# The second layer's rotation table, made in the first layer's expert stage

## The chip, the cores and the metric

The kernel runs on one core of one Trainium2 chip. Its engines are TensorE (PE in the profile, its weight loads PEld), VectorE (DVE), ScalarE (ACT), GpSimd (POOL) and SyncE (SP, which issues nearly all DMAs). Each engine takes its instructions strictly in the order in which they stand in its queue. The metric is device time in microseconds (us); lower is better. Before the change three runs took 1702.73, 1703.41 and 1704.15 us, a median of 1703.41 us.

## The reference

Two layers work on 256 latent tokens (`x`) and 256 context tokens (`ctx`), width 1024. Each layer has a mixer (three parallel parts: an S5 state-space scan, latent attention and a Hyena long convolution) and then a mixture of 32 SwiGLU experts, of which each token goes to two:

```python
for i in range(DEPTH):                       # DEPTH = 2
    u, cq, ckv, kr, hz = split(modulate(x, norm1_g[i], ...) @ w_in[i])
    s5  = s5_mixer(u, lam[i], b[i], c[i])    # h[t] = lam_bar*h[t-1] + bu[t], complex, both directions
    mla = mla_mixer(cq, ckv, kr, ...)
    hy  = hyena_mixer(hz, filters[i])
    x   = x + gate * (merge_groups(s5, mla, hy) @ w_out[i])
    x   = x + gate2 * hier_moe(modulate(x, norm2_g[i], ...), w1[i], w3[i], w2[i])
return rms_norm(x, final_g)
```

`lam_bar = exp(lam * dt)` depends on weights alone, and so do its powers. The second layer returns only the latent tokens.

## The kernel before

Every 128x1024 buffer is a "page" out of a pool of 44. Both mixers are written as Python generators that are woven into each other: each `yield` hands over to the next generator, and a scheduler, which works from a simulated timeline, then fixes every engine's queue. The expert stage is different: it stands inside a region with a manual schedule (`moe`, from L1763 on), where the instructions stay in the order in which they are written.

**The scan and its table.** `s5_scan` (L855 to L874) works on chunks of eight tokens, 64 chunks for each of 16 groups. It turns the complex recurrence into a real one: the driving values are multiplied by a table of rotations (cosines and sines, two pages), scanned with real decays `rho` (one page), and turned back. `s5_rotation` makes these. First, from the angle's cosine and sine, it squares and renormalises small 128x2x16 tiles eight times (`square`, L473 to L475, three DVE instructions; `unit`, L339 to L342, four, after six of the squarings), and squares the magnitude three times (L487). Then it doubles the table five times (L503 to L508), six DVE instructions for each length, 2 to 32 for each of the 16 groups, so 32 to 512 elements a partition. One ACT copy spreads the decays over the `rho` page. All of it hangs on weights alone.

**Where it is called.** Each mixer weaves four generators, named by letters in `first`: r the rotation, d the drive matrices (`expand`, L436 to L445 on DVE, whose results PE transposes at L460), c the scan's input chunks, a the inputs of the attention (L789, L939). In the first mixer the order of the letters is 'rdca', in the second 'acrd', with d empty there: the second layer's drive matrices are made earlier, in the first layer's expert stage.

**The expert stage of the first layer.** For each of 32 experts, 12 pages of weights (512 KB each) come in through SP; PE multiplies 64 gathered tokens by eight of them (`first_half`, L1586), ACT and DVE make SwiGLU of it (L1592 on DVE), PE turns it (`turn`, L1601) and multiplies by the other four (`second_half`, L1610), ACT and DVE scale the result (L1722), and PE adds it back to the tokens (`combine`, L1692), with a DVE addition into `xT` for each bank of PSUM (`residual`, L1624). A comparison (L1873) makes the matrix of ones and zeros that the next `combine` needs. After the 32 experts comes one more block for an expert with over 64 tokens (`first_half(X1, pages)`), then the last additions (`combine_last`, L1702), and a loop over further such blocks whose count is read from memory (L1905).

**Steps for the second layer in this stage.** `next_weights` chains generators of the second layer, and the stage takes one step of it twice for each expert from the seventh on (`NAHEAD` is 6). What is left after the 32nd expert is taken at once by `for _ in ahead: pass`. Between two `yield`s stands one step.

**The limit on weights ahead.** `ws.pump` says how many pages may be written into the program ahead of the page in use: 34 less the expert's number, but not under `NLAST`.

```python
            if e >= NAHEAD:
                next(ahead, None)      # stands twice in each expert
        for _ in ahead:                # after expert 31
            pass
        if i == 0:
            b = first_half(X1, pages)
```

Of the kernel before, what the change touches and what calls it, by code (L numbers as in the profile page):

```python
# [31 lines left out]
BIG = 1.0e30  # L32
NPAGE = 44
NEARLY = 5
NFIRST, NSTEP, NLAST, NAHEAD = 34, 1, 18, 6
PLAN = [
    {'lag': 2, 'ts': True, 'vs': False, 'nbank': (3, 3, 2), 'kvs': True,
     'qs': True, 'ps': True, 'order': 'ahsd', 'na': 1, 'ro': 2,
# [32 lines left out]
def build(tc, A, dbg=None):  # L71
# [8 lines left out]
    stage = ["z"]  # L80
# [209 lines left out]
    def layer_weights(i):  # L290

        V = {}
# [173 lines left out]
        def s5_rotation():  # L466

            stage[0] = "S5r"
            E = small([128, 6, 2, 16])
            mag = X["mag"]  # L470

            def square(d, a):
                nc.vector.tensor_mul(X["usq"][:, 0:2], a, a)  # L473
                nc.vector.scalar_tensor_tensor(d[:, 1], a[:, 0], 2.0, a[:, 1], op0=OP.mult, op1=OP.mult)
                nc.vector.tensor_sub(d[:, 0], X["usq"][:, 0], X["usq"][:, 1])  # L475

            e2 = small([128, 2, 16])
            e4 = small([128, 2, 16])
            square(e2, X["z"][:, 3:5])
            square(e4, e2)  # L480
            square(E[:, 0], e4)
            unit(E[:, 0])
            for n in range(5):
                square(E[:, n + 1], E[:, n])
                unit(E[:, n + 1])
            for _ in range(3):
                nc.vector.tensor_mul(mag, mag, mag)  # L487
            yield
            stage[0] = "S5r"
            T = [page(), page()]  # L490
            x = page()
            Tv = [t.rearrange("p (g s) -> p g s", g=16) for t in T]
            xv = x.rearrange("p (r g s) -> p r g s", r=2, g=16)
            nc.gpsimd.memset(Tv[0][:, :, 0:1], 1.0)
            nc.gpsimd.memset(Tv[1][:, :, 0:1], 0.0)
            for j in range(2):
                nc.vector.tensor_copy(Tv[j][:, :, 1:2], E[:, 0, j, :, None])
            for l in range(1, 6):
                n = 1 << l
                b_r, b_i = (E[:, l, j, :, None].to_broadcast([128, 16, n]) for j in range(2))  # L500
                a_r, a_i = Tv[0][:, :, 0:n], Tv[1][:, :, 0:n]
                o_r, o_i = Tv[0][:, :, n:2 * n], Tv[1][:, :, n:2 * n]
                nc.vector.tensor_mul(o_r, a_r, b_r)  # L503
                nc.vector.tensor_mul(xv[:, 0, :, 0:n], a_i, b_i)
                nc.vector.tensor_mul(o_i, a_r, b_i)
                nc.vector.tensor_mul(xv[:, 1, :, 0:n], a_i, b_r)
                nc.vector.tensor_sub(o_r, o_r, xv[:, 0, :, 0:n])
                nc.vector.tensor_add(o_i, o_i, xv[:, 1, :, 0:n])  # L508
            rho = page()
            rv = rho.rearrange("p (g s) -> p g s", g=16)  # L510
            act(rv, mag[:, :, None].to_broadcast([128, 16, 64]), AF.Copy)
            nc.gpsimd.memset(rv[:, :, 0:1], 0.0)
            V["rot"] = T
            V["rho"] = rho
            yield
# [64 lines left out]
        def s5_readout_matrices():  # L580
# [52 lines left out]
            for tau in range(8):  # L633
                for x in range(2):
# [6 lines left out]
                 readout=s5_readout_matrices)  # L641
# [106 lines left out]
    def mixer(i, acc):  # L748
# [10 lines left out]
        V = V_[i]  # L759
# [38 lines left out]
        def s5_chunks(u):  # L798

            stage[0] = "S5b"  # L800
            half = halves()
            Ut = [half(), half()]
            for t4 in range(2):
                b = bank(side=True)
                for t in range(4):
                    for m in range(2):
                        nc.tensor.matmul(b[64 * m:64 * m + 64, t * 128:(t + 1) * 128], u[m][:, t4 * 4 + t:512:8], ident,
                                         start=True, stop=True, tile_position=(0, 64 * m))
                bv = b.rearrange("p (t g h) -> p g t h", t=4, g=8)
                for g4 in range(2):  # L810
                    nc.scalar.copy(Ut[g4].rearrange("p (g t h) -> p g t h", g=4, t=8)[:, :, t4 * 4:t4 * 4 + 4, :],
                                   bv[:, g4 * 4:g4 * 4 + 4])
            yield
            stage[0] = "S5b"
            U = [half(), half()]
            for g4 in range(2):
                b = bank(side=True)
                for g in range(4):
                    nc.tensor.transpose(b[:, g * 128:(g + 1) * 128], Ut[g4][:, g * 128:(g + 1) * 128], ident)
                nc.scalar.copy(U[g4], b)  # L820
            V["U"] = U
            yield
# [461 lines left out]
        if i == 0:  # L1284
# [14 lines left out]
            spectrum = V["spectrum"]()  # L1299
# [8 lines left out]
        else:  # L1308
            rstd1 = rstd_of(None, D, acc=acc)
            first_projections(rstd1)  # L1310
            ahead(1)
        first = dict(r=V["rotation"], d=V["drive"] if i == 0 else lambda: iter(()), c=lambda: s5_chunks(V["u"]), a=attention_inputs)
        weave(*(first[c]() for c in pl["first"]), spectrum if i == 0 else iter(()))
        ro = V["readout"]() if i == 0 else iter(())
        n, mid = pl["ro"], pl["mid"]
# [89 lines left out]
    def moe(i, pctx, router, ws, last_part):  # L1405
# [394 lines left out]
        def next_weights():  # L1800

            V = V_[1]
            V["bank"] = lambda: pb("pX", 2)
            for name in ("spectrum", "powers", "readout", "drive"):
                for _ in V[name]():
                    stage[0] = "MOE"
                    yield
# [275 lines left out]
```

## Time and profile before

| | before |
|---|---|
| median of 3 runs | 1703.41 us |
| the profiled execution, its own time | 1700.06 us |
| its span, first to last instruction | 1698.2 us |
| PE, DVE, ACT, POOL busy | 1526.5, 890.3, 482.8, 95.6 us |
| mean granted TensorE clock | 0.955 of 2.4 GHz |
| DMA | 505.84 MB, mean 298 GB/s |

The profile's 40 slices of 42.5 us tell the stages apart. The first mixer lies in the first ten (DMA at 36 to 237 GB/s in most of them, PE and DVE taking turns), the first layer's experts in slices 10 to 21 (DMA at about 408 GB/s), the second mixer in slices 22 to 27 or so (36 to 300 GB/s, the granted clock down to six tenths in slice 22), the second layer's experts after that, again at 409 GB/s. The times in the rows are microseconds from the span's start; "[4.94 <-ACT MOEh L119]" at a row's end means that the engine was idle for 4.94 us before it, and that an ACT instruction at line 119 (the helper that issues all activations), writing MOEh, ended that. Names begin with the stage that made the tile: S5a, S5r and S5s for the scan, MOE for the experts, QKV and PROJ for the attention's inputs and the projections.

### The profile page before, as it was taken

What the parts mean: (1) busy time and instruction counts of PE and PEld (TensorE: products, weight loads), DVE (VectorE), ACT (ScalarE), POOL (GpSimd) and SP (SyncE); (2) the same over time, 40 slices, a digit from 0 to 9 for tenths busy, and PEclk for the clock granted to TensorE, in tenths of its full rate; (3) what the DMA queues carried; (4) which work ended last, traced back from release to release, by engine and by line L of the source; (5) the groups of instructions that cost most, each with busy time, mean ns of one, the idle gap of its engine ahead of it and who ended that gap; (6) DMA issues with size and microseconds to landing.
All of it is one profiled execution on the core that took longest, in us unless ns stands there. A gap on an engine that the chain in (4) does not pass through costs nothing. (4 is left out here: it accounts for less than half of the span.)

```text
span 1698.2 us, 22546 instructions
## 1 busy us (share of the span) xinstructions
PE 1526.5 (90%) x8073; PEld 785.7 (46%) x8073; DVE 890.3 (52%) x2180; ACT 482.8 (28%) x931; POOL 95.6 (6%) x154
## 2 busy tenths in 40 slices
PE   5888889997999999999999588898799999999985
PEld 1676744475433333344333477547444444333322
DVE  6769565555244546873744757455534444333233
ACT  3343545442111122111122534445311111111112
POOL 0000212002000000001100000010100000000000
PEclk9998899999999999999999698999899999999998
DMA  9111254659999999999999112578699999999994
GB/s 345 64 37 63 75 186 153 234 209 345 353 382 406 409 409 408 407 408 387 346 408 403 36 58 100 214 265 302 257 391 409 409 409 409 409 409 409 409 409 174
DMA packets 143300, 505.84 MB, mean 298 GB/s; under 512 B 19021, under 2 KB 19599, under 8 KB 142928
## 3 DMA queue, kind: packets, MB, share of 16 engines
q1 hardware_dynamic: 138736, 495.21, 75.6%
q0 software_dynamic: 4160, 8.61, 1.6%
q8 instruction: 66, 1.08, 0.3%
q10 hardware_dynamic: 288, 0.52, 0.1%
q14 instruction: 50, 0.41, 0.1%
HBM read 504.85 MB, written 3.64 MB: 299 GB/s over the span
## 5 line engine op out<-in xcount | busy, mean ns | idle before, releaser
L1586 PE MATMUL MOEp<-MOEpg,MOEpg 128*64 128x512 f32 x956 | 227.7, 603 | 13.6 <-DMA MOEpg<-in_w 12.4
L1722 DVE SCALAR_TENSOR_TENSOR MOEpg<-MOEpY,MOEwt,MOEpg 64x512 fp32r<-64x512 f32 x128 | 95.9, 749 | 243.6 <-ACT MOEpg L119 243.5
L1610 PE MATMUL MOEpY<-MOEpg,MOEhT 128*64 128x512 f32 x960 | 220.9, 602 | 1.8 <-DVE MOEhT L1602 1.8
L1586 PE MATMUL MOEp<-MOEpg,ROUTpg 128*64 128x512 f32 x960 | 215.5, 598 | 1.2 <-DMA MOEpg<-in_w 1.1
L1624 DVE SCALAR_TENSOR_TENSOR zxT<-MOEpC,zmod,zxT 128x256 f32<-128x256 f32 x385 | 168.1, 478 | 8.9 <-PE MOEpC L1702 2.8
L119 ACT ACTIVATE MOEpg<-MOEpY,MOEwt 64x512 fp32r<-64x512 f32 x128 | 87.4, 683 | 278.5 <-PE MOEpY L1610 220.5
L1592 DVE TENSOR_TENSOR MOEh<-MOEh,MOEp 128x256 f32<-128x256 f32 x65 | 27.3, 420 | 233.2 <-ACT MOEh L119 233.1
L1692 PE MATMUL MOEpC<-MOEGT,MOEpg 128*128 128x512 f32 (+1 forms) x496 | 130.1, 364 | 6.8 <-DVE zxT L1624 5.9
L119 ACT ACTIVATE MOEh<-MOEp 128x256 f32<-128x256 f32 x65 | 25.0, 385 | 388.5 <-PE MOEp L1586 388.5
L1586 PEld LDWEIGHTS MOEp<-MOEpg,MOEpg 128*64 128x64 f32 x956 | 59.2, 136 | 160.2 <-DMA MOEpg<-in_w 91.6
L1586 PEld LDWEIGHTS MOEp<-MOEpg,ROUTpg 128*64 128x64 f32 x960 | 65.5, 137 | 136.8 <-issue 105.2
L1610 PEld LDWEIGHTS MOEpY<-MOEpg,MOEhT 128*64 128x64 f32 x960 | 64.0, 137 | 121.6 <-issue 96.3
L1692 PEld LDWEIGHTS MOEpC<-MOEGT,MOEpg 128*128 128x128 f32 x496 | 75.2, 189 | 61.7 <-issue 26.0
L167 PE MATMUL ADAb<-ADApg,zcact 128*32 128x512 f32 x384 | 75.0, 614 | 12.2 <-DMA ADApg<-in_adaw 12.2
L789 PE MATMUL PROJb<-INPpg,PROJpg 128*128 128x512 f32 (+1 forms) x384 | 73.8, 356 | 6.4 <-DVE PROJpg L975 5.7
L789 PEld LDWEIGHTS PROJb<-INPpg,PROJpg 128*128 128x128 f32 x384 | 63.5, 206 | 15.9 <-ACT PROJpg L119 6.7
L119 ACT ACT_TABLE_LOAD x35 | 44.9, 1283 | 15.6 <-DVE ATTst L1103 5.7
L1661 PE MATMUL MOEpG<-MOEpg,ROUTpg 128*128 128x256 f32 x240 | 44.6, 310 | 1.1 <-DVE MOEpg L1496 1.1
L1661 PEld LDWEIGHTS MOEpG<-MOEpg,ROUTpg 128*128 128x128 f32 x240 | 33.0, 193 | 24.2 <-issue 15.8
L1374 PE MATMUL OUTb<-OUTpg,ATTpg 128*128 128x512 f32 (+1 forms) x192 | 39.1, 362 | 1.2 <-DVE ATTpg L231 1.2
L1092 PE MATMUL ATTb<-QKVpg,QKVpg 96*128 96x512 f32 x64 | 34.2, 637 | 6.5 <-ACT ATTpg L119 6.5
L1708 POOL TENSOR_TENSOR zxT<-zxT,MOEpg 128x512 f32<-128x512 f32 (+1 forms) x6 | 6.0, 1001 | 534.7 <-ACT MOEpg L119 534.6
(544 smaller groups left out, 2143.4 us busy)
## 6 DMA issues: line engine op xcount, KB each, us to landing
MOEpg<-in_w SPq DMA_DIRECT2D x719, 512.0 KB, 10.2
ADApg<-in_adaw SPq DMA_DIRECT2D x96, 512.0 KB, 6.9
ROUTpg<-in_w SPq DMA_DIRECT2D x61, 512.0 KB, 5.8
PROJpg<-in_win SPq DMA_DIRECT2D x16, 512.0 KB, 3.2
ATTpg<-in_wout SPq DMA_DIRECT2D x8, 512.0 KB, 3.3
OUTpg<-in_wout SPq DMA_DIRECT2D x8, 512.0 KB, 4.4
QKVpg<-in_uq SPq DMA_DIRECT2D x5, 512.0 KB, 3.3
MOEpg<-in_win SPq DMA_DIRECT2D x5, 512.0 KB, 10.1
```

What stands on the lines that cost most here:

```text
L119: nc.scalar.activation(out, in_, f, **kw)
L167: nc.tensor.matmul(b[q:q + 32, :], cact[:, k, :], w[:, h * 512:(h + 1) * 512], start=(k < 2), stop=(k >= KD - 2), tile_position=(0, q))
L789: nc.tensor.matmul(b, a_[:, c], b_[k][:, c0:], start=(first and n == 0), stop=(last and n == 2))
L1092: nc.tensor.matmul(b, qc[h][:, nq - NS + qt * 128:nq - NS + (qt + 1) * 128], kc[h], start=True, stop=True)
L1374: nc.tensor.matmul(b, a_[:, c], y_, start=(n == 0 and j == 0), stop=(n == KD - 1 and j == 2))
L1586: nc.tensor.matmul(b[64 * h:64 * h + 64, :], X[:, k, :], w[:, h * 512:(h + 1) * 512], start=(k == 0), stop=(k == KD - 1), tile_position=(0 ...
L1592: nc.vector.tensor_mul(h_, h_, b[:, 256:512])
L1610: nc.tensor.matmul(b[64 * h:64 * h + 64, :], hT[:, k % 2, (k // 2) * 64:(k // 2) * 64 + 64], w[:, h * 512:(h + 1) * 512], start=(k == 0), ...
L1624: nc.vector.scalar_tensor_tensor(xT[:, k, seg(s)], b[:, s * NS - c0:(s + 1) * NS - c0], mod[:, 40 + k, s:s + 1], xT[:, k, seg(s)], op0=OP. ...
L1661: nc.tensor.matmul(b[:, kk * 256:(kk + 1) * 256], hs[t][:, k * 128:(k + 1) * 128], G[:, t].rearrange("p e c -> p (e c)"), start=(t == 0 an ...
L1692: nc.tensor.matmul(b, Y_[p][j][rows, k * 128:(k + 1) * 128], GT_[p][rows], start=(j == 0), stop=(j == 1))
L1722: nc.vector.scalar_tensor_tensor(Y[1][rows_of, h * 512:(h + 1) * 512], b[rows], wt[rows], yh.bitcast(F32), op0=OP.mult, op1=OP.subtract)
```

## The change

`rotation` is added to the list that `next_weights` chains, at its end; the second mixer's r becomes empty. `s5_rotation` gets a `yield` ahead of each of five squarings and of each of the five doublings, which holds in the first mixer too. `NLAST` falls from 18 to 14.

```diff
--- before.py
+++ after.py
@@ -32,7 +32,7 @@
 BIG = 1.0e30
 NPAGE = 44
 NEARLY = 5
-NFIRST, NSTEP, NLAST, NAHEAD = 34, 1, 18, 6
+NFIRST, NSTEP, NLAST, NAHEAD = 34, 1, 14, 6
 PLAN = [
     {'lag': 2, 'ts': True, 'vs': False, 'nbank': (3, 3, 2), 'kvs': True,
      'qs': True, 'ps': True, 'order': 'ahsd', 'na': 1, 'ro': 2,
@@ -481,6 +481,8 @@
             square(E[:, 0], e4)
             unit(E[:, 0])
             for n in range(5):
+                yield
+                stage[0] = "S5r"
                 square(E[:, n + 1], E[:, n])
                 unit(E[:, n + 1])
             for _ in range(3):
@@ -496,6 +498,8 @@
             for j in range(2):
                 nc.vector.tensor_copy(Tv[j][:, :, 1:2], E[:, 0, j, :, None])
             for l in range(1, 6):
+                yield
+                stage[0] = "S5r"
                 n = 1 << l
                 b_r, b_i = (E[:, l, j, :, None].to_broadcast([128, 16, n]) for j in range(2))
                 a_r, a_i = Tv[0][:, :, 0:n], Tv[1][:, :, 0:n]
@@ -1309,7 +1313,7 @@
             rstd1 = rstd_of(None, D, acc=acc)
             first_projections(rstd1)
             ahead(1)
-        first = dict(r=V["rotation"], d=V["drive"] if i == 0 else lambda: iter(()), c=lambda: s5_chunks(V["u"]), a=attention_inputs)
+        first = dict(r=V["rotation"] if i == 0 else lambda: iter(()), d=V["drive"] if i == 0 else lambda: iter(()), c=lambda: s5_chunks(V["u"]), a=attention_inputs)
         weave(*(first[c]() for c in pl["first"]), spectrum if i == 0 else iter(()))
         ro = V["readout"]() if i == 0 else iter(())
         n, mid = pl["ro"], pl["mid"]
@@ -1801,7 +1805,7 @@
 
             V = V_[1]
             V["bank"] = lambda: pb("pX", 2)
-            for name in ("spectrum", "powers", "readout", "drive"):
+            for name in ("spectrum", "powers", "readout", "drive", "rotation"):
                 for _ in V[name]():
                     stage[0] = "MOE"
                     yield
```

Lines of the changed kernel are 2 to 4 higher than those of the kernel before.

**VectorE at the end of the first layer's experts.** Here L1722 and L1624 belong to expert 31, L1873 makes its matrix MOEGT, and the first L1592 after it is the SwiGLU product of the additional block, MOEh. Before:

```order
L1722 SCALAR_TENSOR_TENSOR MOEpg_6787<-MOEpY_6875,MOEwt_6137,MOEpg_6786 64x512 x2
L1624 SCALAR_TENSOR_TENSOR zxT_84<-MOEpC_6888,zmod_69,zxT_84 128x256 x2
L1873 TENSOR_SCALAR MOEGT_6893<-ziotaN_85,MOEidx_6135 128x512
L1592 TENSOR_TENSOR MOEh_6918<-MOEh_6918,MOEp_1469_6901 128x256
L1624 SCALAR_TENSOR_TENSOR zxT_84<-MOEpC_6922,zmod_69,zxT_84 128x256 x2
L1624 SCALAR_TENSOR_TENSOR zxT_84<-MOEpC_6927,zmod_69,zxT_84 128x256 x2
L1904 MEMSET MOEk_3290 128x1
```

Now, the same place up to the first instructions of the rotation (L473 to L475 are a squaring on S5a):

```order
L1726 SCALAR_TENSOR_TENSOR MOEpg_6779<-MOEpY_6869,MOEwt_6129,MOEpg_6778 64x512 x2
L1628 SCALAR_TENSOR_TENSOR zxT_84<-MOEpC_6888,zmod_69,zxT_84 128x256 x2
L1877 TENSOR_SCALAR MOEGT_6893<-ziotaN_85,MOEidx_6127 128x512
L473 TENSOR_TENSOR S5apg_3839<-S5apg_3839 128x32
L474 SCALAR_TENSOR_TENSOR S5apg_5075<-S5apg_3839 128x16
L475 TENSOR_TENSOR S5apg_5075<-S5apg_3839 128x16
L473 TENSOR_TENSOR S5apg_3839<-S5apg_5075 128x32
```

and where that ends (L511 and L512 close the last doubling, on S5r, L1596 is the SwiGLU product):

```order
L507 TENSOR_TENSOR S5rpg_6952<-S5rpg_6952,S5apg_5075 128x16x32
L508 TENSOR_TENSOR S5rpg_6954<-S5rpg_6953,S5apg_5075 128x512
L509 TENSOR_TENSOR S5rpg_6953<-S5rpg_6952,S5apg_5075 128x16x32
L510 TENSOR_TENSOR S5rpg_6954<-S5rpg_6953,S5apg_5075 128x512
L511 TENSOR_TENSOR S5rpg_6952<-S5rpg_6952,S5rpg_6954 128x16x32
L512 TENSOR_TENSOR S5rpg_6953<-S5rpg_6953,S5rpg_6954 128x16x32
L1596 TENSOR_TENSOR MOEh_7009<-MOEh_7009,MOEp_1473_6992 128x256
L1628 SCALAR_TENSOR_TENSOR zxT_84<-MOEpC_7013,zmod_69,zxT_84 128x256 x2
L1628 SCALAR_TENSOR_TENSOR zxT_84<-MOEpC_7018,zmod_69,zxT_84 128x256 x2
```

All 83 instructions of the rotation, 81 rows from L473 to L512, stand in one piece between MOEGT and the SwiGLU product of the additional block; none stands in an earlier expert.

**VectorE in the second mixer, ahead of the scan.** L231 is the low half of a projection's weights, L503 to L508 the last doublings, L855 the scan's first product, on S5s. Before:

```order
L231 TENSOR_TENSOR PROJpg_7672<-PROJpg_7669,PROJpg_7671 128x1024
L507 TENSOR_TENSOR S5rpg_7629<-S5rpg_7629,S5rpg_7631 128x16x16
L508 TENSOR_TENSOR S5rpg_7630<-S5rpg_7630,S5rpg_7631 128x16x16
L503 TENSOR_TENSOR S5rpg_7629<-S5rpg_7629,S5apg_5075 128x16x32
L505 TENSOR_TENSOR S5rpg_7630<-S5rpg_7629,S5apg_5075 128x16x32
L504 TENSOR_TENSOR S5rpg_7631<-S5rpg_7630,S5apg_5075 128x512
L506 TENSOR_TENSOR S5rpg_7631<-S5rpg_7630,S5apg_5075 128x512
L231 TENSOR_TENSOR PROJpg_7704<-PROJpg_7701,PROJpg_7703 128x1024
L507 TENSOR_TENSOR S5rpg_7629<-S5rpg_7629,S5rpg_7631 128x16x32
L508 TENSOR_TENSOR S5rpg_7630<-S5rpg_7630,S5rpg_7631 128x16x32
L855 TENSOR_TENSOR S5spg_7763<-S5spg_7735,S5rpg_7630 128x512
L856 TENSOR_TENSOR S5spg_7762<-S5spg_7735,S5rpg_7629 128x512
```

Now:

```order
L231 TENSOR_TENSOR PROJpg_7627<-PROJpg_7624,PROJpg_7626 128x1024
L231 TENSOR_TENSOR PROJpg_7672<-PROJpg_7669,PROJpg_7671 128x1024
L231 TENSOR_TENSOR PROJpg_7704<-PROJpg_7701,PROJpg_7703 128x1024
L862 TENSOR_TENSOR S5spg_7763<-S5spg_7735,S5rpg_6953 128x512
L859 TENSOR_TENSOR S5spg_7763<-S5spg_7735,S5rpg_6953 128x512
L860 TENSOR_TENSOR S5spg_7762<-S5spg_7735,S5rpg_6952 128x512
L861 TENSOR_TENSOR S5spg_7762<-S5spg_7735,S5rpg_6952 128x512
```

The doublings are gone; the scan's first products follow the weights' splits.

**VectorE in the first mixer.** L436 to L445 make the drive matrices, L503 to L508 (L507 to L512 in the changed kernel) double the table. Before, with the table's last doubling ahead of most of the drive matrices:

```order
L503 TENSOR_TENSOR S5rpg_655<-S5rpg_655,S5apg_292 128x16x32
L505 TENSOR_TENSOR S5rpg_656<-S5rpg_655,S5apg_292 128x16x32
L504 TENSOR_TENSOR S5rpg_657<-S5rpg_656,S5apg_292 128x512
L506 TENSOR_TENSOR S5rpg_657<-S5rpg_656,S5apg_292 128x512
L231 TENSOR_TENSOR PROJpg_720<-PROJpg_717,PROJpg_719 128x1024
L576 TENSOR_TENSOR PROJpg_649<-SPECpg_749,SPECb_653 128x512
L577 TENSOR_TENSOR PROJpg_649<-SPECpg_749,SPECb_653 128x512
L436 TENSOR_TENSOR SPECpg_757<-S5apg_292,S5apg_253 128x512
L438 TENSOR_TENSOR SPECpg_757<-S5apg_292,S5apg_253 128x512
L507 TENSOR_TENSOR S5rpg_655<-S5rpg_655,S5rpg_657 128x16x32
L508 TENSOR_TENSOR S5rpg_656<-S5rpg_656,S5rpg_657 128x16x32
L231 TENSOR_TENSOR PROJpg_765<-PROJpg_762,PROJpg_764 128x1024
```

Now, with the last drive matrices ahead of all but the first doubling:

```order
L437 TENSOR_TENSOR S5apg_550<-S5apg_292,S5apg_253 128x512
L438 TENSOR_TENSOR S5rpg_806<-S5apg_292,S5apg_253 128x512
L439 TENSOR_TENSOR S5apg_552<-S5apg_292,S5apg_253 128x512
L441 TENSOR_TENSOR S5apg_550<-S5apg_550,S5rpg_782 128x512
L445 TENSOR_TENSOR S5apg_552<-S5apg_552,S5rpg_782 128x512
L507 TENSOR_TENSOR S5rpg_799<-S5rpg_799,S5apg_292 128x16x2
L509 TENSOR_TENSOR S5rpg_800<-S5rpg_799,S5apg_292 128x16x2
L508 TENSOR_TENSOR S5rpg_801<-S5rpg_800,S5apg_292 128x16x2
L510 TENSOR_TENSOR S5rpg_801<-S5rpg_800,S5apg_292 128x16x2
L441 TENSOR_TENSOR S5apg_550<-S5apg_550,S5rpg_806 128x512
L445 TENSOR_TENSOR S5apg_552<-S5apg_552,S5rpg_806 128x512
L511 TENSOR_TENSOR S5rpg_799<-S5rpg_799,S5rpg_801 128x16x2
```

Before, the table's 32 instructions stood ahead of the last three of the four pairs of L441 and L445; now 26 of them stand behind the last pair.

## Rows read from the trace of the kernel before

**Rows 1.** Stretches: width, busy time by engine (instructions), PEclk, DMA share, GB/s.

```profile
900.00:920.00 20.00, 19.56 (x98) 8.08 (x96) 6.62 (x14) 4.40 (x8) 0.00 (x0) 1.00 1.03 409
...
940.00:960.00 20.00, 9.98 (x28) 7.49 (x28) 13.35 (x25) 12.93 (x21) 3.82 (x3) 0.50 0.05 15
```

**Rows 2.** Timeline of DVE, end of the first layer's experts: start, duration, instruction.

```profile
922.57 0.48 DVE L1873 TENSOR_SCALAR MOEGT<-ziotaN,MOEidx 128x512 fp32r<-128x512 f32 x1
927.98 0.42 DVE L1592 TENSOR_TENSOR MOEh<-MOEh,MOEp 128x256 f32<-128x256 f32 x1 [4.94 <-ACT MOEh L119]
928.32 1.65 DVE L1624 SCALAR_TENSOR_TENSOR zxT<-MOEpC,zmod,zxT 128x256 f32<-128x256 f32 x4
```

**Rows 3.** Timeline of PE, the same place.

```profile
927.45 1.19 PE L1692 MATMUL MOEpC<-MOEGT,MOEpg 128*128 128x512 f32 x4
929.33 0.70 PE L1692 MATMUL MOEpC<-MOEGT,MOEpg 128*128 128x512 f32 x2 [0.69 <-DVE zxT L1624]
...
932.52 3.65 PE L1610 MATMUL MOEpY<-MOEpg,MOEhT 128*64 128x512 f32 x16
...
940.74 2.04 PE L1702 MATMUL MOEpC<-MOEGT,MOEpg 64*128 64x512 f32 x4 [3.42 <-DVE zxT L1624]
```

**Rows 4.** Timeline of DVE, squarings of the second layer among the first layer's experts.

```profile
702.54 0.19 DVE L342 TENSOR_TENSOR S5apg<-S5apg,S5apg 128x32 f32<-128x32 f32 x1
702.76 0.19 DVE L473 TENSOR_TENSOR S5apg<-S5apg 128x32 f32<-128x32 f32 x1
...
703.20 0.19 DVE L339 TENSOR_TENSOR S5apg<-S5apg 128x32 f32<-128x32 f32 x1
...
703.84 0.19 DVE L342 TENSOR_TENSOR S5apg<-S5apg,S5apg 128x32 f32<-128x32 f32 x1
```

**Rows 5.** Stretches, instructions on the table (S5rpg) alone; both mixers.

```profile
77.00:98.00 21.00, 9.00 (x32) 1.05 (x1) 0.13 (x1) 1.00 0.08 27
...
1001.00:1015.00 14.00, 9.40 (x33) 1.05 (x1) 0.12 (x1) 0.98 0.20 71
```

**Rows 6.** Timeline of DVE, second mixer, the scan.

```profile
1014.43 0.69 DVE L855 TENSOR_TENSOR S5spg<-S5spg,S5rpg 128x512 f32<-128x512 f32 x1
...
1022.69 0.17 DVE L206 RECIPROCAL QKVrs<-QKVrs 128x4 f32<-128x4 f32 x1
```

**Rows 7.** Timeline of ACT, second mixer, ahead of the scan.

```profile
1005.63 1.05 ACT L119 ACTIVATE S5rpg<-S5apg 128x1024 f32<-128x1024 f32 x1
1006.58 1.99 ACT L119 ACTIVATE PROJpg<-PROJpg 128x1024 fp32r<-128x1024 f32 x2
1008.47 2.49 ACT L119 ACTIVATE S5spg<-S5sb 64x504 f32<-64x504 f32 x6
...
1014.18 0.26 ACT L119 ACTIVATE QKVrs<-QKVb,zeps 128x4 f32<-128x4 f32 x1 [2.05 <-PE QKVb L202]
```

**Rows 8.** Timeline of PE, second mixer, the same place.

```profile
1005.15 7.26 PE L841 MATMUL S5sb<-S5bpg,S5bpg 128*128 128x64 f32 x64
...
1022.91 1.11 PE L218 MATMUL QKVb<-zident,QKVrs 128*128 128x128 f32 x4 [8.77 <-DVE QKVrs L206]
```

**Rows 9.** Timeline of PE, first mixer, transposes of the drive matrices and what follows.

```profile
107.23 1.11 PE L460 MATMUL S5bb<-zident,S5apg 128*128 128x128 f32 x4 [3.34 <-DVE S5apg L441]
108.52 4.50 PE L460 MATMUL S5bb<-zident,S5apg 128*128 128x128 f32 x20 [0.18 <-DVE S5apg L441]
112.82 3.98 PE L841 MATMUL S5sb<-S5bpg,S5bpg 128*128 128x64 f32 x32
```

**Rows 10.** Timeline of DVE, first mixer, its first wait after that.

```profile
123.92 1.41 DVE L986 SCALAR_TENSOR_TENSOR S5bpg<-S5bpg,zchp,QKVb 128x512 f32<-128x512 f32 x2 [4.88 <-PE QKVb L218]
```

**Rows 11.** Stretch of the first mixer, columns as in the first group.

```profile
110.00:114.00 4.00, 4.00 (x24) 4.00 (x22) 0.00 (x0) 3.20 (x7) 0.00 (x0) 0.57 0.00 0
```

**Rows 12.** Waits of the weights' queue, 600 to 940 us: total, times, longest.

```profile
SPq L115 <- DMA MOEpg<-in_w: 229.9, 240, 4.0
...
SPq L115 <- PE MOEpY L1610: 4.3, 15, 0.4
```

## The prediction

> **What bounds the kernel now.** I read the slices of the page first: the first layer's experts and the second layer's run at about 409 GB/s, the mixers at far less. The windows then say what limits each stage. In the last experts of the first layer PE is busy 19.56 of 20 us while the DMA share is 1.03, and DVE only 6.62 [rows 1]: a page of 512 KB every 1.28 us (524288 bytes over 409 GB/s), twelve for an expert, 15.4 us an expert. The queue of the weights waits there 229.9 us in 240 pieces for transfers that it issued before, and 4.3 us in 15 pieces for the matmuls that free a page [rows 12]. So the experts are fed by memory, and small work on DVE beside them costs nothing as long as PE's inputs come in time. At the stage's end it is another matter. The weights have run out, the same two windows show the clock at half and DMA at 0.05 [rows 1], and every engine waits for one other in turn: a delay there is passed on in full. In both mixers PE, DVE and ACT take turns as well, and the waits in the timelines say who comes last.
>
> **Where the rotation goes.** The words of the change say "in steps among the experts". The queues say otherwise. The stage takes two steps in each of 26 experts (7 to 32), 52 in all, and the four generators that stood in the list before have 13, 8, 15 and 16 yields, 52 too. The rotation comes fifth, so none of its steps is reached, and all are emitted by the loop that empties the chain after expert 31. VectorE's queue shows 83 instructions in one piece between MOEGT and the SwiGLU product of the additional block. Queues are in order, so that product waits for all 83.
>
> **Term 1, the piece at the end of the experts.** Its length, from this trace: a squaring with its renormalising has seven instructions and takes 1.30 us (703.84 less 702.54), a bare squaring 0.44 (703.20 less 702.76) [rows 4]. Six of the first, two of the second and three squarings of the magnitude at 0.2 make 7.80 + 0.88 + 0.60 = 9.28 us. The table, 32 instructions, was busy 9.00 us in the first mixer, 9.40 with the scan's first instruction in the second [rows 5]; I take 9.0. Together 18.3 us. It starts where MOEGT ends (922.57 + 0.48 = 923.05) and ends at 941.3. The product started at 927.98 before, after 4.94 us of idle time on DVE that ACT's Silu ended [rows 2]: those 4.94 us hide part of the piece, the other 13.3 us do not. Nothing else hides it. Behind the product stand on DVE the additions into xT (L1624), for which PE's combine waits (0.69 us already), on PE the turn, second_half and the last combine [rows 3]; the SyncE loop (L1905) and the second mixer's normalisation follow from them.
>
> Then the clock. PE can do the first two banks of the combine and then stops for some 13 us. In the profile PE's clock is at half after waits far shorter than that: it waited 3.34 us in the first mixer, and 110 to 114 us were granted 0.57 [rows 9, 11]; after 3.42 us at the end of the experts [rows 3] the stretch was at 0.50 [rows 1]. So after 13 us of idleness the eight combine matmuls that stand from 929.33 to second_half (the first two are in a row) run at half clock, 0.51 us each as at 940.74 (2.04 over 4) instead of 0.30 as at 927.45 (1.19 over 4) [rows 3]: 8 x 0.21 = 1.7, less some 0.3 of PE's waiting between them that this fills (its 0.69 at 929.33 is one such wait), 1.4 us. In the first mixer the clock was at half from 107.23 to about 113.4 (0.57 over 4 us leaves 0.56 us at full speed), 6.2 us after PE's resumption [rows 9, 11]. Here second_half begins about 5 us after it, so about 1.2 of its 3.65 us [rows 3] are at half clock, 0.6 us. Term 1: 13.3 + 1.4 + 0.6 = **+15.3 us**. Ends: 13.0 with a table of 8.7 (9.40 less the 0.69 of L855 [rows 5, 6]) and no loss by the clock; 18.7 with the whole of second_half at half clock (13.3 + 1.7 + 3.65).
>
> A rule that speaks for a lower price stands in the Trainium skill, "Perfetto Trace Analysis", Identifying the Most-Contended Engine: for Vector the occupancy is a fair measure of how near the engine is to its limit. By it 18.3 us on an engine that is busy a third of the time would be free, and the term 0. The trace's row speaks against it at this place, since the idle time of the experts lies ahead of the piece in the queue; I give it the chance of rival B.
>
> **Term 2, the first mixer.** The new yields hold there too. The weaving takes one step from each generator in turn, and 26 of the table's 32 instructions now stand behind the drive matrices. PE waited 3.34 and 0.18 us for these (L441), and then ran 20 transposes in 4.30 us (112.82 less 108.52) at half clock [rows 9]. With the table behind, about 8 us of DVE work leave the way of L441; I keep 0.8 of the 3.52 us of waiting, as ACT's and DVE's first instructions of each matrix are still due, and gain 2.7. Without that wait the clock need not fall; the transposes then gain 1.9 (most of half of 4.30). Sum **-4.6 us**. DVE must be ready that much sooner for its next work behind PE; it waited 4.88 us there [rows 10], which covers it, barely. Ends: 0, if another wait takes its place, and -5.4 (3.52 + 1.9).
>
> **Term 3, the second mixer.** The table (9.0 us on DVE) and rho (1.05 on ACT [rows 7]) leave the stretch ahead of the scan. The scan started at 1014.43 behind the table, and PE waited 8.77 us for the reciprocal QKVrs, which stands behind the scan at 1022.69 [rows 6, 8]. What is late next: the scan's inputs are copied by ACT out of PSUM. These copies (2.49 us for six) began at 1008.47 behind two splits of 1.99 us that began at 1006.58, behind rho; without rho these begin at 1005.63 [rows 7], the copies about 0.95 sooner, and the chunks that the scan needs first are there about 1010.1 by the copies' pace and PE's L841, which runs until 1012.41 [rows 8]. The scan then starts 4.3 us sooner instead of 10, and so does the reciprocal, whose input is ready at 1014.18 [rows 7] and hence does not hold it. **-4.3 us**. Ends: 0, and -10.05, the whole of table and rho.
>
> **Edits at nothing.** The small squarings stood inside the experts before, where the scheduler had moved them; they leave 9.3 us of DVE work there, behind a stage fed by memory: 0, hidden as it was by the pages' pace. `NLAST` from 18 to 14 lets four pages fewer be written ahead in the last experts. The queue waits for transfers that are out already, not for its place in the program [rows 12], so 0; at the other end four pages of 1.28 us, +5.1, if each came late once. Gains below 0 have no source, since a shorter list ahead issues no page sooner.
>
> **Sum.** 15.3 - 4.6 - 4.3 = +6.4 us. Against the profiled execution, 1700.06 us (span 1698.2), this gives 1706.5; that execution lies 3.35 us below the median of 1703.41, so the forecast for a median is **1709.8 us**. The three terms' ends, not all at once, give 1705.5 to 1713.5 for this case.
>
> **Rivals.** A: the second mixer gives back the whole table and rho, 10.05 us instead of 4.3. For it: PE waits 8.77 us in one piece there and DVE is what it waits for [rows 6, 8]; against it: ACT's copies and L841 go on until after 1010 [rows 7, 8]. Sum 15.3 - 4.6 - 10.05 = +0.65: 1704.1 us, no change.
> B, the other side: the piece is hidden after all, as if it lay in DVE's idle time in the experts. For it: DVE is busy 6.62 of 20 us [rows 1]; against it: the order on DVE, with only 4.94 us of idle time behind MOEGT [rows 2]. Only -4.6 - 4.3 = -8.9 is left: 1694.5 us. It decides as soon as term 1 is under 5.5 us.
> C: the shorter limit on pages ahead makes PE wait for weights at the end of the stage, +5.1 more: 1714.9 us. For it: the stage has no slack at a DMA share of 1.03 [rows 1]; against it: the queue's waits [rows 12].
> D: both mixers only shift their waits, and term 1 stands alone: 1718.7 us. For it: DVE's cover in the first mixer is barely enough [rows 10], and after the scan comes the same chain as before; against it: two waits of PE (3.34 and 8.77) that end on instructions directly behind the table [rows 8, 9].
>
> **Chances.** The forecast 66%, of which 6 lie within 0.2% of before (3.4 us, about what a measurement of this kernel can tell from no change); A 13%, B 5%, C 8%, D 8%. Slower by more: 60 + 8 + 8 = 76%; within: 6 + 13 = 19%; faster: 5%. The range takes in A and half of C and leaves B and D out: 1702.5 to 1715.5 us.
>
> **What would show it.** Right: on DVE some 18 us of small S5a and S5r instructions behind MOEGT, the SwiGLU product about 13 us later, PE idle meanwhile and its clock at half at the turn; the experts as long as before and the same waits of the weights' queue; PE's wait for QKVrs at 4 to 5 us instead of 8.77; PE's wait for L441 under 1 us and the clock at full from 106 to 114 us. Wrong: the product no more than 5 us late (B), a stretch of PE waiting for pages after expert 25 (C), a wait of unchanged length under another name in a mixer (D), or the scan starting as soon as 1004 on the old scale (A).

## The result, and the profile after

The median rose from 1703.07 us (6 runs, 1700.58 to 1704.15) to 1710.23 us (6 runs, 1709.06 to 1711.41): ratio 1.0051, 95% interval 1.0040 to 1.0062. By the medians this is +7.2 us, where +6.4 had been forecast; by the ratio it is +8.7, from 6.8 to 10.6. The profiled execution took 1709.95 us, near its median (span 1708.1); that of before lay 3 us under its own, so the two traces differ by more (9.9 us) than the medians do. A stretch where they drift apart without the change is shown below.

All instructions of the rotation run in one piece at the end of the first layer's experts. VectorE's timeline there, as in [rows 2]:

```profile
916.00 0.48 DVE L1877 TENSOR_SCALAR MOEGT<-ziotaN,MOEidx 128x512 fp32r<-128x512 f32 x1
916.39 0.18 DVE L473 TENSOR_TENSOR S5apg<-S5apg 128x32 f32<-128x32 f32 x1
...
933.69 0.70 DVE L512 TENSOR_TENSOR S5rpg<-S5rpg,S5rpg 128x512 f32<-128x512 f32 x1
934.29 0.43 DVE L1596 TENSOR_TENSOR MOEh<-MOEh,MOEp 128x256 f32<-128x256 f32 x1
```

The SwiGLU product follows MOEGT after 18.29 us (934.29 less 916.00); before it was 5.41 (927.98 less 922.57 [rows 2]). The difference, 12.88 us, is the part of the piece that shows; the other 5 us are hidden by the idle time that VectorE had at this place before (4.94 us [rows 2]), called the cover below. TensorE at the same place, answering to [rows 3]:

```profile
920.90 1.19 PE L1696 MATMUL MOEpC<-MOEGT,MOEpg 128*128 128x512 f32 x4
935.65 1.19 PE L1696 MATMUL MOEpC<-MOEGT,MOEpg 128*128 128x512 f32 x2 [13.55 <-DVE zxT L1628]
...
940.30 3.90 PE L1614 MATMUL MOEpY<-MOEpg,MOEhT 128*64 128x512 f32 x16
```

Two banks of the combine, then 13.55 us of waiting, then second_half 6.01 us behind the product (940.30 less 934.29) instead of 4.54 (932.52 less 927.98): 1.47 us more. In windows, with columns as in [rows 1], the experts still ran at the memory's pace (DMA share 1.03), and in the gap TensorE did nothing and its granted clock fell (1.00 is 2.4 GHz, 0.50 is 1.2 GHz, its two levels; a value between them is a stretch with some of each):

```profile
900.00:920.00 20.00, 19.32 (x91) 6.95 (x88) 10.08 (x37) 3.29 (x6) 0.25 (x2) 1.00 1.03 408
922.00:935.50 13.50, 0.10 (x1) 0.00 (x0) 12.86 (x56) 2.90 (x4) 0.13 (x1) 0.69 0.43 174
```

In the first mixer the waits of [rows 9] for the drive matrices fell from 3.34 and 0.18 us to 0.54 and 0.99, and L845 (L841 before) started 5.81 us sooner:

```profile
103.11 0.63 PE L460 MATMUL S5bb<-zident,S5apg 128*128 128x128 f32 x4 [0.54 <-DVE S5apg L441]
104.73 2.45 PE L460 MATMUL S5bb<-zident,S5apg 128*128 128x128 f32 x20 [0.99 <-DVE S5apg L441]
107.01 3.78 PE L845 MATMUL S5sb<-S5bpg,S5bpg 128*128 128x64 f32 x32
...
117.26 0.60 PE L218 MATMUL QKVb<-zident,QKVrs 128*128 128x128 f32 x4
```

The second mixer came 8.12 us later and left its first wait 3.74 us later: 4.38 us were gained. On PE (answering to [rows 8]), then on ACT and on DVE (to [rows 7] and [rows 6]):

```profile
1013.27 7.25 PE L845 MATMUL S5sb<-S5bpg,S5bpg 128*128 128x64 f32 x64
...
1026.65 1.11 PE L218 MATMUL QKVb<-zident,QKVrs 128*128 128x128 f32 x4 [4.39 <-DVE QKVrs L206]
```

```profile
1016.16 2.51 ACT L119 ACTIVATE S5spg<-S5sb 64x504 f32<-64x504 f32 x6 [0.41 <-PE S5sb L845]
```

```profile
1018.77 0.69 DVE L859 TENSOR_TENSOR S5spg<-S5spg,S5rpg 128x512 f32<-128x512 f32 x1 [0.59 <-ACT S5spg L119]
...
1026.42 0.17 DVE L206 RECIPROCAL QKVrs<-QKVrs 128x4 f32<-128x4 f32 x1
```

The scan's products now wait for ACT's copies, no longer for the table. One of the four (L862) runs at 1017.49, the next (L859) at 1018.77 after 0.59 us for ACT; less 8.12 these are 1009.37 and 1010.65 on the old scale, where 1010.1 had been worked out.

**Some 3 us that are not the change's.** From that first wait to a matmul of the attention (1144.23 before, 1148.95 after) the traces come apart by about 1 us more (3.74 to 4.72), and from there to the output projection by another 3 us, in the same instructions. Windows of ten us, of before and then of after:

```profile
1144.00:1154.00 10.00, 8.98 (x60) 5.27 (x55) 7.51 (x20) 5.26 (x14) 0.00 (x0) 1.00 0.92 343
```

```profile
1148.72:1158.72 10.00, 10.00 (x51) 6.23 (x47) 5.86 (x15) 3.32 (x8) 0.00 (x0) 0.66 0.65 251
```

TensorE's clock stayed at full in the one (1.00) and went to half for most of the other (0.66). The kernels of the experiments show both pictures without any change there: against the profile of before, e1, e2, e4, e8, e9 and a second profile of the changed kernel lose 3 to 4.5 us between that matmul and the output projection, e3, e5, e6, e7, e10 and e11 0.2 us or less. So it goes with the single execution and not with the change, and it is likely one reason why the runs of one kernel spread over 1 to 9 us here. In the output projection about 1.9 us more are lost in the same way (clock 0.83 in the changed kernel from 1168.72 to 1188.72, 1.00 before from 1164 to 1184).

### The profile page after: what moved, and what is told of

The parts are those of the page before. It is cut to its first block, busy times and chain, and to the rows that moved or that the text cites. A ratio compares the mean times of both kernels' runs of the same rounds, so it can differ in the third digit from the quotient of the medians.

```text
span 1708.1 us, 22542 instructions
## 1 busy us (share of the span) xinstructions
PE 1530.7 (90%) x8073; PEld 787.8 (46%) x8073; DVE 893.1 (52%) x2180; ACT 482.3 (28%) x931; POOL 95.7 (6%) x154
## 5 line engine op out<-in xcount | busy, mean ns | idle before, releaser
L1596 DVE TENSOR_TENSOR MOEh<-MOEh,MOEp 128x256 f32<-128x256 f32 x65 | 27.4, 421 | 229.8 <-ACT MOEh L119 229.7
L167 PE MATMUL ADAb<-ADApg,zcact 128*32 128x512 f32 x384 | 75.9, 615 | 13.3 <-DMA ADApg<-in_adaw 13.3
L1378 PEld LDWEIGHTS OUTb<-OUTpg,ATTpg 128*128 128x128 f32 x192 | 34.5, 213 | 5.1 <-DVE ATTpg L231 0.2
## 6 DMA issues: line engine op xcount, KB each, us to landing
MOEpg<-in_w SPq DMA_DIRECT2D x719, 512.0 KB, 10.2
```

The lines of the kernel that those rows point to most:

```text
L167: nc.tensor.matmul(b[q:q + 32, :], cact[:, k, :], w[:, h * 512:(h + 1) * 512], start=(k < 2), stop=(k >= KD - 2), tile_position=(0, q))
L1378: nc.tensor.matmul(b, a_[:, c], y_, start=(n == 0 and j == 0), stop=(n == KD - 1 and j == 2))
L1596: nc.vector.tensor_mul(h_, h_, b[:, 256:512])
```

## The experiments

Each was timed in five rounds against the kernel before, on one chip with it. Its runs of before had medians of 1701.8 to 1702.9 us. The first line is the result above. The ratio is that to the kernel before, and need not be the quotient of the two medians:

| kernel | median, us | ratio, 95% interval |
|---|---|---|
| changed | 1710.23 | 1.0051 (1.0040 to 1.0062) |
| changed, again | 1712.54 | 1.0068 (1.0052 to 1.0085) |
| e1 spread | 1695.08 | 0.9952 (0.9938 to 0.9966) |
| e2 first mixer alone | 1699.20 | 0.9984 (0.9974 to 0.9994) |
| e3 old first mixer | 1711.49 | 1.0051 (1.0038 to 1.0064) |
| e4 NLAST 18 | 1711.30 | 1.0047 (1.0034 to 1.0060) |
| e5 spread, drive first | 1694.11 | 0.9963 (0.9949 to 0.9976) |
| e6 table left | 1701.42 | 1.0006 (0.9995 to 1.0018) |
| e7 spread, scan first | 1699.96 | 0.9995 (0.9986 to 1.0005) |
| e8 PE busy for 9.9 us | 1713.38 | 1.0055 (1.0036 to 1.0075) |
| e9 as e5, PE's waits filled | 1695.19 | 0.9961 (0.9946 to 0.9976) |
| e10 PE busy for 13.5 us | 1709.18 | 1.0036 (1.0023 to 1.0049) |
| e11 as e5, narrow run broken | 1694.62 | 0.9960 (0.9947 to 0.9973) |

**e1: the steps truly spread.** A third step in each of the last 14 experts:

```diff
                 if e >= NAHEAD:
                     next(ahead, None)
+                if e >= NE - 14:
+                    next(ahead, None)
                 stage[0] = "MOE"
```

> The changed kernel with one more step of the chain in each of the last 14 experts, so that the rotation's steps are all taken inside the experts and none is left after expert 31. Theory (the piece of 83 instructions ahead of the SwiGLU product costs what the trace shows, 14.3 us from the first combine to second_half): 1710.2 - 14.3 = 1696 us, give or take 2; the product comes about 5 us after MOEGT again and PE's wait of 13.55 us is gone. Rival (small DVE work is not free inside the experts, since it delays products there or pages that the steps take are missing from the weights): PE waits appear in experts 18 to 31, and 1700 to 1708 us.

1695.08 us, as the theory had it. VectorE at the end of the experts:

```profile
919.65 0.48 DVE L1877 TENSOR_SCALAR MOEGT<-ziotaN,MOEidx 128x512 fp32r<-128x512 f32 x1
925.26 0.42 DVE L1596 TENSOR_TENSOR MOEh<-MOEh,MOEp 128x256 f32<-128x256 f32 x1 [5.13 <-ACT MOEh L119]
```

Its last experts, columns as in [rows 1]:

```profile
900.00:920.00 20.00, 19.13 (x88) 6.51 (x88) 15.31 (x35) 4.55 (x7) 0.12 (x1) 1.00 1.03 408
```

The product is 5.61 us behind MOEGT again. Inside the stage the products of experts 21 and 22 (counted from 0) came up to 4.8 us later than in the changed kernel, and at expert 28 nothing of that was left (0.03 us): there the pages set the pace, and the added DVE work, up to 15.31 busy us of 20, was free in the end. This kernel beats both others; 15 us by the medians (14.2 in the traces from MOEGT to second_half) lie between it and the changed one, by where 83 instructions stand in a queue. The third step also brings the last steps of the other four generators forward, which this run does not tell apart.

**e6: a shorter piece.** As e1, with `NE - 7` for `NE - 14`, so that the last squaring and the table remain behind MOEGT.

> The spread kernel with the extra step in the last 7 experts instead of 14, so that only the last squaring and the table stand in a piece behind MOEGT: 1.3 + 0.6 + 8.6 = 10.5 us instead of 18. Theory of the in-order queue with 4.94 us of cover: the product is 10.5 - 4.9 = 5.6 us late, and PE's wait costs 1 to 1.5 us more by its clock: 1695.1 + 6.5 to 7 = 1702 us. Rival (what costs is PE's falling clock, whatever the length of the wait): nearly the whole 14 us, 1709 us. Rival (no cover, the piece costs its length): 1705.6 us.

1701.42 us, 6.3 over e1 (7.3 over e5, which was timed beside it), as the theory of the covered queue has it.

```profile
917.16 0.48 DVE L1877 TENSOR_SCALAR MOEGT<-ziotaN,MOEidx 128x512 fp32r<-128x512 f32 x1
...
927.85 0.41 DVE L1596 TENSOR_TENSOR MOEh<-MOEh,MOEp 128x256 f32<-128x256 f32 x1
```

10.69 us instead of 5.41, so 5.3 of the piece's 10.3 us show. Of the 17.9 us in the changed kernel (916.39 to 934.29) 12.9 show: two lengths give the same cover of 5 us.

**e8 and e10: TensorE kept busy during the wait.** Matmuls that compute nothing needed, 42 in e8 and 57 in e10:

```diff
-                combine(last, range(0, 3))
+                combine(last, range(0, 2))
+                idle = pb("pY", 1)
+                for _ in range(42):
+                    nc.tensor.matmul(idle[:, 0:n], Y_[last][0][:, 0:128], GT_[last], start=True, stop=True)
+                combine(last, range(2, 3))
```

> The changed kernel with 42 matmuls that compute nothing needed (the combine's operands into a bank that second_half overwrites) between PE's second and third bank of the last combine, 12.6 us at 0.30 us each, so that PE is not idle while VectorE works off the piece. Theory (13 us of the cost are the queue, and some 1.5 us the half clock after the wait): the product still comes 18.3 us after MOEGT, the clock stays at full, and second_half starts 4.5 us behind the product as before the change instead of 6.0; the time is 1.5 us below the changed kernel. Rival (the piece itself is slowed or the clock is irrelevant): second_half 6.0 us behind the product as in the changed kernel.

They took 0.236 us each and not 0.30, so PE still waited 3.78 us, the clock fell, and second_half stayed 6.00 us behind the product (938.59). The 0.30 was a misreading: each matmul starts before the last one has ended, so 1.19 us over four counts the tail of the fourth as well; in that row too the trace has the later starts 0.23 us apart. This run cannot tell the theory from its rival:

```profile
926.23 9.92 PE L1900 MATMUL MOEpY<-MOEGT,MOEpg 128*128 128x512 f32 x42
939.93 1.19 PE L1696 MATMUL MOEpC<-MOEGT,MOEpg 128*128 128x512 f32 x2 [3.78 <-DVE zxT L1628]
...
944.59 4.15 PE L1614 MATMUL MOEpY<-MOEpg,MOEhT 128*64 128x512 f32 x16
```

> As e8 with 57 matmuls instead of 42, since each took 0.236 us there (9.92 over 42) and 3.78 us of waiting were left: 57 x 0.236 = 13.5 us fill the whole wait. Theory: PE waits under 0.5 us, the clock stays at full, second_half starts 4.5 to 4.9 us behind the product instead of 6.0; the time is 1 to 1.5 us below the changed kernel, less than a median can tell, so the trace decides. Rival: second_half stays 6.0 us behind the product though the clock is at full.

With the wait filled the theory held. TensorE, then the product on VectorE:

```profile
924.00 13.46 PE L1900 MATMUL MOEpY<-MOEGT,MOEpg 128*128 128x512 f32 x57
937.71 0.70 PE L1696 MATMUL MOEpC<-MOEGT,MOEpg 128*128 128x512 f32 x2 [0.25 <-DVE zxT L1628]
...
940.90 3.65 PE L1614 MATMUL MOEpY<-MOEpg,MOEhT 128*64 128x512 f32 x16
```

```profile
936.37 0.41 DVE L1596 TENSOR_TENSOR MOEh<-MOEh,MOEp 128x256 f32<-128x256 f32 x1
```

940.90 less 936.37 is 4.53 us, as before the change; two combine matmuls take 0.70 us as in [rows 3] and not 1.19. So up to second_half 1.47 us of the piece's price are the clock, and 12.9 the queue. In the other profiles with the full piece and an unfilled wait, second_half stands 5.7 to 6.0 us behind the product, so the clock's part is 1.2 to 1.5 us. The median, 1709.18, agrees but is too near the changed kernel's to show it.

**e4: the limit on pages.** `NLAST` back at 18.

> The changed kernel with NLAST at 18 again. Theory (the weights' queue waits for its own transfers, not for its place in the program): 1710.2 us, give or take 1. Rival C of the prediction (four pages come late): 1705 us, and waits of PE for pages gone in experts 25 to 31.

1711.30 us; its interval and that of the changed kernel overlap almost whole, so rival C is out. The weights' queue of the changed kernel, 600 to 945 us, as in [rows 12]:

```profile
SPq L115 <- DMA MOEpg<-in_w: 224.1, 234, 3.3
...
SPq L115 <- PE MOEpY L1614: 2.3, 9, 0.3
```

**e2 and e3: the first mixer alone, and all but it.** In e2 the yields stand in the kernel before under `if i == 0:`; in e3 those of the changed kernel under `if i:`.

> The kernel before with the new yields in the first mixer alone; the second layer's rotation stays in the second mixer and NLAST at 18. Theory (the first mixer's gain is the 5.8 us by which L841 starts sooner in the changed kernel, and it passes through the experts): 1703.1 - 5.8 = 1697.3 us. Rival (the expert stage is fed by memory and its weights come no sooner, so the gain is lost there): 1703 us.

> The changed kernel without the yields in the first mixer. Theory (terms add): 1710.2 + 5.8 = 1716 us, the piece and the second mixer as in the changed kernel. Rival (the first mixer's gain was used up later): 1710 us.

Both missed. e2 gained 2.8 us, not 5.8, and e3 lost nothing against the changed kernel. The traces show where it goes. Two profiles of the changed kernel, same stretches (columns as in [rows 1]), the first run and then the second:

```profile
108.00:112.00 4.00, 4.00 (x39) 4.00 (x37) 4.00 (x10) 3.35 (x8) 0.00 (x0) 1.00 0.40 131
112.00:116.00 4.00, 4.00 (x21) 3.39 (x21) 1.17 (x3) 0.33 (x2) 0.15 (x2) 1.00 0.00 0
116.00:120.00 4.00, 4.00 (x22) 3.29 (x21) 2.11 (x4) 1.30 (x3) 0.00 (x0) 1.00 0.18 41
```

```profile
108.00:112.00 4.00, 4.00 (x38) 4.00 (x38) 4.00 (x10) 3.35 (x8) 0.00 (x0) 1.00 0.34 117
112.00:116.00 4.00, 4.00 (x16) 3.47 (x16) 1.76 (x4) 0.86 (x3) 0.15 (x2) 0.56 0.04 14
116.00:120.00 4.00, 4.00 (x12) 3.15 (x11) 0.00 (x0) 0.00 (x0) 0.00 (x0) 0.59 0.00 0
```

In the first the clock stays at full and the 5.8 us are kept: the first expert's product comes 5.50 us sooner. In the second it falls at 112 us and the product comes 1.15 us sooner. The same instructions of PE, from L845 to the first L218, take 10.25 us in the first (117.26 less 107.01, above) and 13.45 in the second:

```profile
107.53 3.78 PE L845 MATMUL S5sb<-S5bpg,S5bpg 128*128 128x64 f32 x32
...
120.98 0.60 PE L218 MATMUL QKVb<-zident,QKVrs 128*128 128x128 f32 x4
```

The nine profiles of e1, e2 and e4 to e10 show the second picture, more or less (0.50 to 0.88 from 112 to 116 us), with 0.8 to 4.7 us left at the first expert; the stretch from L845 to L218 takes 11.84 to 11.88 us in seven of them and 13.46 to 13.48 in two. So the fall of the clock that the old order had at 107 to 113 us [rows 9, 11] was put off, and seldom avoided.

**e5, e9 and e11: why the clock falls in the first mixer.** e5 is e1 with 'drca' for 'rdca'; e9 adds five transposes of no use ahead of the third and the fourth group at L460.

> The spread kernel (e1) with the letters of the first mixer as 'drca' instead of 'rdca', so that the drive matrices stand ahead of all doublings. Theory: PE's two waits that are left there (0.54 and 0.99 us) let the clock fall in some executions, which costs 3.3 us near the reciprocal and is why e2 gave 2.8 us and not 5.8. With the matrices a step sooner the second wait is under 0.5 us, the clock stays at full and the time is 1.5 to 3 us below e1, 1692 to 1693.5. Rival (those waits come from ACT's copies and DVE's products of the matrices themselves, not from the table): same as e1 within 1 us.

> The kernel e5 (spread, drive matrices first) with five transposes that compute nothing needed ahead of the third and of the fourth group of the drive matrices' transposes on PE, 0.6 us each time, where PE waits 0.54 and 0.58 us. Theory (these waits make the clock fall from 112 us on in some executions, which takes back 1.5 to 4 us of the first mixer's gain): the waits are gone, the clock is at 1.00 from 100 to 124 us, QKVrs of the first mixer comes 6 us sooner than in the kernel before, and the time is 1 to 3 us below e5, 1691 to 1693. Rival (the fall of the clock comes of waits elsewhere or of nothing in the program's order): the clock falls at 112 us all the same and the time is that of e5.

e5 is 1694.11 us, the same as e1 within the noise; the clock falls to 0.57 from 112 to 116 us in its profile. e9 took the waits away, and the clock fell all the same, so those waits are not needed for the fall. PE, and the windows behind it:

```profile
105.81 1.47 PE L463 MATMUL S5bb<-zident,S5apg 128*128 128x128 f32 x12
107.54 1.14 PE L463 MATMUL S5bb<-zident,S5apg 128*128 128x128 f32 x8 [0.25 <-ACT S5bpg L465]
108.52 3.78 PE L848 MATMUL S5sb<-S5bpg,S5bpg 128*128 128x64 f32 x32
112.14 1.90 PE L202 MATMUL QKVb<-zones,QKVpg 128*128 128x2 f32 x16
```

```profile
112.00:116.00 4.00, 4.00 (x26) 3.63 (x26) 2.93 (x6) 1.49 (x4) 0.15 (x2) 0.86 0.28 101
116.00:120.00 4.00, 4.00 (x14) 3.18 (x14) 0.00 (x0) 0.00 (x0) 0.00 (x0) 0.71 0.00 0
```

PE had no wait over 0.25 us there. By the 0.86 the clock fell at about 114.9 us, some 0.8 us after the end of 32 matmuls of 64 columns and 16 of 2. e11 leaves e5's waits as they are and breaks this run with two matmuls that compute nothing needed:

```diff
+        if nch == 256 and not dense:
+            dense.append(1)
+            for _ in range(2):
+                nc.tensor.matmul(b[:, 0:512], acc[0][:, 0:128], acc[0][:, 0:512], start=True, stop=True)
         for j, sq in enumerate(acc):
```

> The kernel e5 with two matmuls of 512 columns that compute nothing needed, between the 32 matmuls of 64 columns (L845 of the changed kernel) and the 16 of 2 columns (L202) in the first mixer. They cost TensorE some 2 us. Theory (what precedes the fall of the clock at 112 to 115 us is the run of narrow matmuls, not a wait): with the run broken the clock stays at 1.00 from 100 to 124 us, and the 2 us are paid back by the 1.5 to 4 us that the fall takes, so the time is that of e5 or up to 2 us less. Rival (the fall hangs on the waits ahead of the transposes at L460, which e9 filled with transposes only, or on the moment alone): the clock falls all the same, and the time is 1 to 2 us above e5.

The clock stayed at full, with PE's waits of 0.54 and 0.58 us still there:

```profile
107.15 3.78 PE L851 MATMUL S5sb<-S5bpg,S5bpg 128*128 128x64 f32 x32
110.77 1.94 PE L205 MATMUL QKVb<-QKVpg 128*128 128x512 f32 x4
112.54 1.84 PE L208 MATMUL QKVb<-zones,QKVpg 128*128 128x2 f32 x16
```

```profile
112.00:116.00 4.00, 4.00 (x26) 3.35 (x25) 1.59 (x4) 0.47 (x2) 0.15 (x2) 1.00 0.00 1
116.00:120.00 4.00, 4.00 (x21) 3.34 (x20) 0.24 (x1) 0.00 (x0) 0.00 (x0) 1.00 0.00 0
```

It is one profile, and one of the eleven others with these yields (the changed kernel's first) kept its clock with the same narrow run unbroken. So the narrow run does not bring the fall every time, and that breaking it keeps the clock is suggested and not shown; what makes the clock fall there stays open. The time is that of e5: with the filling PE takes 11.96 us from L851 to the first L218, in e5 11.88 with the fall.

**e7: the scan's inputs ahead of the attention's.** e1 with 'card' for 'acrd' in the second mixer.

> The spread kernel with the letters of the second mixer as 'card' instead of 'acrd', so that the scan's input chunks stand ahead of the attention's inputs. Theory (with the table gone, what is late at the scan is ACT's copies of the chunks behind its splits): the scan and the reciprocal behind it start 1 to 3 us sooner, PE's wait of 4.39 us shrinks by as much, 1692 to 1694 us. Rival (PE's wait is then ended by another chain, since the norm's columns come later by the same change): same as e1 or slower.

The rival was right: 1699.96 us, 5 more than e1. Counted from the SwiGLU product of the additional block, L845 begins 4.8 us sooner than in e1, but PE then waits 3.49 us in its midst for ACT to empty a bank, and the norm's sums (L202) come 6.1 us later, and so the reciprocal 5.7 us later:

```profile
1010.17 3.44 PE L845 MATMUL S5sb<-S5bpg,S5bpg 128*128 128x64 f32 x16 [3.49 <-ACT S5spg L119]
1013.39 3.52 PE L202 MATMUL QKVb<-zones,QKVpg 128*128 128x2 f32 x16
1019.36 1.12 PE L218 MATMUL QKVb<-zident,QKVrs 128*128 128x128 f32 x4 [2.45 <-DVE QKVrs L206]
```

**The changed kernel again.**

> The changed kernel once more, on the chip of the three others, for their ratio and for a second profile. Theory: 7 to 9 us above before; in the first mixer the profile shows either the clock at full up to 120 us and L845 some 5.8 us sooner than before with all of it kept, or, as in e1, half clock from 112 us and 3.3 us of it lost. Rival (the difference between e1 and the changed kernel in the first mixer comes from the code): the same shifts as in its first profile.

1712.54 us; the piece and the second mixer repeat to 0.05 us (12.9 and 4.4), the first mixer does not.

## Why the prediction was right, step by step

- **The rotation in one piece behind MOEGT, nothing of it in the experts**: right, by the rows above. e1, in which the steps do lie in the experts, is rival B made true, and its 1695.08 us are what B's 1694.5 had said. The rule of the Trainium skill ("Perfetto Trace Analysis", Identifying the Most-Contended Engine), by which Vector's occupancy says how near it is to its limit, agrees with e1, where the rotation in the experts, at 15.31 busy us of 20, costs nothing in the end. It does not agree with the changed kernel, where VectorE's idle time in the experts lies ahead of the piece in the queue.
- **The piece's length**: 18.3 us forecast, 17.9 measured (916.39 to 934.29); 13.3 us of delay forecast, 12.9 measured in the two profiles of the changed kernel, in e3, e8 and e10, and 12.8 in e4.
- **The clock behind it**: 1.4 us up to second_half forecast, 1.47 measured and shown by e10 (1.2 in e3 and e4); 0.6 in second_half forecast, 0.25 measured (3.90 us instead of 3.65), 0.07 in the second profile and nothing in e3 and e4. The forecast's 0.30 us for a combine matmul at full clock was the misreading named under e8; it did little harm, as the 0.51 at half clock had the same fault.
- **First mixer, -4.6**: the mechanism was right up to 112 us (waits of 3.52 us down to 1.53, L845 5.8 us sooner). The step that failed is "without that wait the clock need not fall": it falls 5 to 8 us later instead, in the second profile of the changed kernel and in nine of the ten kernels of the experiments that have these yields. Counted in medians the term is -2.8 by e2 and nothing by e3 against the changed kernel, which is about as near as medians tell. VectorE's idle time was read from the wrong wait as well: the 4.88 us in [rows 10] stand behind the reciprocal L206. Ahead of it VectorE was idle for 9.88 us, and the postponed doublings filled these (the last one starts at 112.38, L206 at 112.98 without a wait; in the second profile 0.23 us of idle time are left).

```profile
118.86 0.18 DVE L206 RECIPROCAL QKVrs<-QKVrs 128x4 f32<-128x4 f32 x1 [9.88 <-ACT QKVrs L119]
```

- **Second mixer, -4.3**: measured -4.38 at PE's first wait, and the same in e1, e3, e4, e5 and e6. What is late next was named rightly: ACT's copies, and not the table. These came 0.43 us sooner (1016.16 less 8.12, against 1008.47) and not 0.95, since ACT now waits 0.41 us for PE's L845. Rival A (-10) is out.
- **NLAST and the squarings, nothing**: e4 shows the one. For the other, the time from the first expert's product to MOEGT is 478.3 and 478.7 us in the changed kernel, 479.3 before. The 4.3 us of [rows 12] were one row of several for matmuls that free a page (some 14 us together), which changes nothing. Rival C is out by e4, and rival D by e2 and the second mixer.

The sum by measured terms is 12.9 + 1.5 + 0.25 - 2.8 - 4.4 = +7.4 us with e2's first mixer and +10.2 with e3's; the medians say +7.2 and the ratios +8.7 and +11.6. The forecast of +6.4 was low by the first mixer's clock: 1.8 us by e2, 4.6 by e3. The piece and second_half came out 0.75 us cheaper than forecast, which hides part of that, and single runs of one kernel spread by more, so that the two medians agree to 0.8 us is partly luck.

## What to carry to other kernels

Work that is handed out in steps is where its last step stands: count the steps asked for against the steps there are before believing that it is spread, since the rest falls in one piece at the end, in front of whatever that queue holds next. The price of such a piece is its length less the gap that the engine had at that very place; a low share of busy time elsewhere says nothing on it. Where a change removes a wait of TensorE, count the wait as gained and the full clock behind it only as a chance: here it was kept in one of eleven profiles (e11 aside).

## What the runs showed of the hardware

- The granted clock of the same instructions with the same waits differs between executions of one kernel: 1.00 against 0.56 and 0.59 in the first mixer of the changed kernel. In the attention it was 1.00 before and 0.66 after, in instructions that the change does not touch. Such a fall cost 3.2 us from L845 to L218 in the first mixer (13.45 less 10.25), 1.6 in the profiles where it was shorter (11.84 to 11.88), and 3.0 in the attention.
- It fell although TensorE had no wait over 0.25 us (e9), shortly behind matmuls of 64 and of 2 columns, and stayed at full where wide ones broke that run (e11, one profile). It also fell at a wait of 3.78 us that followed 9.9 us of steady matmuls (e8, second_half 6.00 us behind the product), and not where these were drawn out over the wait (e10, 4.53).
- Matmuls of 128x512 in an unbroken row took 0.236 us each (13.46 over 57). A short row read as length over count gives too much (1.19 over 4 is 0.30), since the tail of its last matmul counts in full.
